# Two transformer blocks on one core: block 2's modulation product moved from the recurrence of block 1 to the spreading of the PEER gates

## The chip, the cores and the metric

The program runs on one core of a Trainium2 chip. The core has TensorE (PE in the profile, with PEld for its weight loads), VectorE (DVE), ScalarE (ACT), GpSimd (POOL) and SyncE (SP). SP issues most of the transfers between HBM and the on-chip memory; ACT and POOL issue some of their own. Each engine carries out its instructions in the order in which they stand in its stream. The metric is device time in microseconds (us), and lower is better.

## What is computed

512 tokens of 1024 features pass through two blocks. What matters here of the reference, cut:

```python
# block 1
mod = (silu(c) @ ada_w + ada_b)
shift1, scale1, gate1, shift2, scale2, gate2 = split(mod, 6)
h = rms_norm(x, norm1_g) * (1 + scale1) + shift1
...                       # attention (8 heads) and RWKV-7 delta rule (8 heads, both directions)
x = x + gate1 * mixed
h2 = rms_norm(x, norm2_g) * (1 + scale2) + shift2
x = x + gate2 * peer_ffn(h2)      # product keys, 16384 single-neuron experts
# block 2
mod = silu(c_2) @ w_ada + b_ada   # [1, 6144], needs c_2 alone
h = rmsnorm(x, norm_mix) * (1 + scale_m) + shift_m
...                       # retention, HGRN, GLA, output projection, experts
```

The modulation product of a block is a row of 1024 numbers times a matrix of 1024 x 6144 in float32 (24 MB). Block 2's needs nothing of block 1, and its result is first read when block 2 begins.

## The kernel before

**Order of the instructions.** The program is written as a sequence of tiles and operations. A scheduler that keeps a timeline of its own then fixes each engine's order; operations under `high_priority` go ahead of the others. [...] A tile pool with `bufs=n` has n buffers for a name or tag: a load into a buffer waits until the last reader of its earlier contents is done.

**Stages.** Times are of the profiled execution, from the span's start: projections of block 1 until 216 us; the recurrence (with the attention and the modulation as fillings) to 705; queries and top 16 of the PEER layer to 870; the spreading of the gates to 1147; the expert products to 2140; block 2.

**Modulation (`ada_parts`, lines 203 to 225).** A generator: each `next()` does one of 12 blocks of 512 columns. A block is 8 products (one for each row tile k of 128), each 32x512 in float32 on 128 rows. Row tile k goes to output partitions 32*(k % 4) on, so four neighbours use four column groups of the array. The weights (`adaw`, line 212) come in loads of two row tiles, 512 KB, with two buffers in the pools `wada2` and `wada3`. Line 214 is the product, `adaps` its PSUM tile. After the last block ACT copies the sum (`adarow`, line 219), PE transposes it (line 222), DVE adds the bias (line 224).

**Recurrence (`rwkv`).** For each of 4 pairs of heads: forward products within chunks of 64 steps (`pa`, `pvy`, `pq`), inverses on the lanes, `solve` (tiles `p`, `pm`, `pr`) for each direction, then `chain` (`pS`, lines 872 and 875), which walks over the 8 chunks, and `finish` (`mps`, `vps`). Pair j's forward stands beside pair j-1's backward work. `fill(j, k)` puts fillings between: `ADA[j][k]` blocks of modulation (8 of block 1, then 12 of block 2), attention steps (`sps`, `ptps`, `po`) and, for j = 4, tiles of the output projection (`zps`).

**Spreading (`spread(tt)`, three times 128 tokens).** A group is four tokens: DVE, POOL and ACT make one-hot tiles `oha` (with the gate) and `ohb`, PE multiplies them (`wps`, line 1169, four products), ACT copies the result into `wst` (line 1175), and every fourth group SP stores 1 MB (`wd`, or `wdr` for the last four). 32 groups make a `spread`. Each of `oha` and `ohb` has four buffers. `select(tt)` makes the indices; its transposes are `selps`. Beside it PE runs the first product (`ups`, 24 matmuls a tile) of 28 expert tiles, from loads `uraw`; POOL makes their low parts `ulo`.

**Expert products.** `vacc` from loads `vraw` (256 KB, four buffers), split by ACT into `vhi`, the rest into `vlo`. Their pools take the space of those of the spreading.

Of the kernel before, what the change touches and what calls it, by code (L numbers as in the profile page):

```python
# [40 lines left out]
def shape_consts():  # L41
    """Constants that depend on shapes alone."""
# [6 lines left out]
    # attention: distance and log of the number of patterns holding the offset  # L49
# [5 lines left out]
    # delta rule masks: two chunks of 64 on the partitions  # L55
# [31 lines left out]
def layout(I):  # L87
    """Data layout only: transposes, reshapes, concatenation."""
# [49 lines left out]
class K:  # L138
    def __init__(s, ctx, tc, nc, A):
# [10 lines left out]
        nc.vector.memset(s.onesD, 1.0 / D)  # L150
        s.mod = [cp.tile([128, 48], F32, name=f"mod{i}") for i in range(2)]
# [21 lines left out]
    def tables(s, after, name="natural_log_exp_and_others"):  # L173
        """one set of tables for what follows an activation, here both of log and exp"""
        with s.tc.issue_after(after.ins):
            s.nc.scalar.preload_act_table_set(name)

    def rsqrt(s, out, x, eps):
        """out = (x + eps) ** -0.5"""
        s.nc.scalar.activation(out, x, AF.Ln, bias=eps)  # L180
        s.nc.scalar.activation(out, out, AF.Exp, scale=-0.5)

    def rsqrt6(s, out, x, tmp, eps=1e-6, bias=None):
        """out = (x + eps) ** -0.5, with a step of Newton's method"""
# [6 lines left out]
    # ---------------------------------------------------------------- modulation  # L191
    def ada_begin(s, which, cname, pool):
        nc = s.nc
        sc = pool.tile([128, 8], F32, name=f"silu{which}")
        s.silu = nc.scalar.activation(sc, s.v(cname, 0, 8), AF.Silu)
        rep = pool.tile([128, 8, 43], F32, name=f"crep{which}")
        nc.gpsimd.memset(rep, 0.0)
        nc.vector.tensor_copy(rep[:, :, 11], sc)
        return rep

    def ada_parts(s, which, wname, bname, rep, lo, n, sel, wp, pp, tags=("mm", "tr"), spaces=None):
        """mod columns of the n column blocks (512 wide) from lo on, a block to each next(), two row tiles to a load.
        Block q goes to row q of each quarter, a quarter for every fourth row tile; its other rows get zeros."""
        nc = s.nc
        kn = 2
# [12 lines left out]
        row = wp().tile([128, 512], F32, name="adarow", bufs=1)  # L218
# [8 lines left out]
    # ------------------------------------------------- normalised, modulated input  # L227
    def rms(s, xT, wp, pp, tag="mm", ps=None):
        """rsqrt(mean(x*x) + eps)"""
# [12 lines left out]
    def modnorm(s, xT, r, gname, which, part, hhi, hlo, wp, keep=None):  # L242
        """h = x * r * (g * (1 + scale)) + shift, split in two parts."""
# [13 lines left out]
    def proj_tile(s, wsrc, hhi, hlo, wp, pp, eng=None, n=KT, tag="mm"):  # L257
        """One 128-column tile of the first n row tiles of h @ w, columns on partitions; returns the PSUM tile."""
# [11 lines left out]
    def out_proj(s, wname, mhi, mlo, xT, gatecol, wp, pp, ms=None, ahead=None, begun=0):  # L270
        """x += gate * (mix @ w) from tile begun on; the mean of its squares into ms; loads that run ahead of what follows"""
# [20 lines left out]
class Banks:  # L292
    """PSUM banks by tag"""
# [7 lines left out]
def block1(s, alloc, after):  # L301
    nc, tc, A = s.nc, s.tc, s.A
    mm = nc.tensor.matmul
    with ExitStack() as c1:
# [9 lines left out]
        sel = s.const("sel4", keep)  # L314
        rep = [s.ada_begin(0, "c", keep), s.ada_begin(1, "c2", keep)]
        s.tables(s.silu)

        with ExitStack() as c2:
# [3 lines left out]
            rest = itertools.chain(s.ada_parts(0, "ada_w", "ada_b", rep[0], 4, 8, sel, wada, P, ("ad", "ad")),  # L322
                                   s.ada_parts(1, "ada_w2", "ada_b2", rep[1], 0, 12, sel, wada, P, ("ad", "ad")))

            def room():
                """pools of what runs beside the recurrence"""
# [16 lines left out]
            def tail(forward):  # L343
                """the output projection of all but the last pair beside the last of the recurrence"""
# [8 lines left out]
                todo["late"] = ca = ExitStack()  # L353
                todo["wa"] = ca.enter_context(tc.tile_pool(name="wada3", bufs=2, side="right"))
# [14 lines left out]
            with ExitStack() as c3:  # L369
# [7 lines left out]
                for _ in s.ada_parts(0, "ada_w", "ada_b", rep[0], 0, 4, sel, lambda: wa, P, spaces=spaces):  # L377
# [5 lines left out]
                # token shift coefficient of the token itself  # L383
# [3 lines left out]
                for ct in [24, 25, 16, 12, 17, 18, 19, 13, 14, 15, 20, 21, 22, 23]:  # L387
# [9 lines left out]
                    if 4 <= j < 8:  # L397
                        # kk: normalised by head
# [45 lines left out]
            # the last pair  # L444
            x, wp, (mhi, mlo) = todo["x"], todo["w"], todo["mix"]
            todo["late"].close()
# [21 lines left out]
ATT = 4, 3, 3, 3     # steps of the attention to each filling  # L468
ADA = ((2, 0, 1, 1), (1, 1, 1, 1), (1, 1, 1, 0), (2, 1, 0, 0), (1, 2, 2, 2))    # parts of the modulation to each filling
OUT = 1, 2, 2, 3, 0  # tiles of the output projection to each filling  # L470


def attention(s, P, ap, qkd, vd, mixd):
    """softmax over the three patterns at once, two heads and 128 queries at a time; a step to each next()"""
# [45 lines left out]
def rwkv(s, c, P, zrd, mixd, kkd, sad, gd, room, fill, tail):  # L520
    """Both directions of the delta rule in chunks of 64 steps; the second runs on reversed time.
    Goes on with every next(): constants, gates, the first pair's decays, and the rest, which yields the last
    pair's part of the mix.

    Partitions hold two heads' features (e, f) or two chunks' steps (c, t).  A product that keeps
    the two apart contracts over all 128 partitions, one operand being zero outside its own half.
    """
# [8 lines left out]
    class Room:  # L536
        """a tile in the pool of its tag"""
# [1633 lines left out]
```

## Time and profile before

| what | value |
|---|---|
| median of 3 runs | 2857.38 us (2854.79 to 2861.47) |
| span of the profiled execution, first to last instruction | 2856.4 us |
| PE busy | 2586.5 us, 91% |
| DVE busy | 1999.3 us, 70% |
| mean granted clock of PE | 0.96 of full speed |

The profile gives no time of the profiled execution beside its span; the span lies between the lowest and the highest run, so what lies around it is small against the spread of the runs. Busy shares are means over stages with different limits, so they are read by stage. In a row of busy times, x is the number of instructions; a float32 matmul is two instructions. The number in brackets behind a row of the timeline is the engine's idle time just before it and what ended it.

### The profile page before, as it was taken

How to read it: one execution, taken by the hardware profiler on the slowest of the kernel's cores; microseconds unless marked ns; L12 is line 12 of the kernel's file. 1: busy time of each engine (PE TensorE's matmuls, PEld its weight loads, DVE VectorE, ACT ScalarE, POOL GpSimd, SP SyncE). 2: the span in 40 equal slices, each digit the busy share in tenths (PEclk: the TensorE clock that was granted, in tenths of full speed). 3: DMA queues.
4: the chain of work that ended last, by engine and by line, in shares of the span. 5: the costliest groups of instructions: out<-in, count | busy, mean ns of one | idle time of the engine just before them, and what ended most of it. 6: DMA issues, size and time to landing. Idle time of an engine off the chain costs nothing. (4 is left out here: it accounts for less than half of the span.)

```text
span 2856.4 us, 44680 instructions
## 1 busy us (share of the span) xinstructions
PE 2586.5 (91%) x16918; PEld 2042.6 (72%) x16918; DVE 1999.3 (70%) x3833; ACT 1059.1 (37%) x1946; POOL 1159.9 (41%) x860
## 2 busy tenths in 40 slices
PE   7999888987996786899999999999998999989995
PEld 4764456645886775889999999999986665654442
DVE  3666567544899999788888887878865467563323
ACT  3344434422434465333333333333333353231121
POOL 0012212121534666887776776776542223200002
PEclk9999999998998899999999999999999999889998
DMA  6528763451312465788888888887672222069984
GB/s 243 176 80 273 214 195 87 146 166 58 106 60 76 124 178 166 275 313 312 304 285 282 290 295 286 299 294 270 208 239 96 80 64 79 4 261 413 414 350 170
DMA packets 257160, 587.84 MB, mean 206 GB/s; under 512 B 48024, under 2 KB 120240, under 8 KB 246448
## 3 DMA queue, kind: packets, MB, share of 16 engines
q1 hardware_dynamic: 201856, 393.71, 40.2%
q0 software_dynamic: 38016, 138.43, 14.2%
q10 hardware_dynamic: 17072, 52.83, 5.0%
q8 instruction: 134, 2.20, 0.3%
q14 instruction: 82, 0.67, 0.1%
HBM read 529.05 MB, written 55.84 MB: 205 GB/s over the span
## 5 line engine op out<-in xcount | busy, mean ns | idle before, releaser
L165 PE MATMUL vacc<-gh,vhi 128*128 128x384 f32 x1024 | 346.6, 339 | 19.3 <-DVE xres L1343 13.9
L165 PE MATMUL ups<-phhi,uhi 128*128 128x384 f32 x1024 | 348.8, 341 | 10.4 <-ACT ge L1007 10.4
L167 PE MATMUL ups<-phhi,ulo 128*128 128x384 f32 x1024 | 348.3, 340 | 5.9 <-POOL ulo L171 4.3
L166 PE MATMUL ups<-phlo,uhi 128*128 128x384 f32 x1024 | 348.2, 340 | 1.0 <-DVE phlo L253 1.0
L166 PE MATMUL vacc<-gl,vhi 128*128 128x384 f32 x1024 | 344.8, 337 | 0.7 <-DVE gl L171 0.7
L167 PE MATMUL vacc<-gh,vlo 128*128 128x384 f32 x1024 | 325.6, 339 | 11.2 <-POOL vlo L171 10.2
L170 ACT ACTIVATE vhi<-vraw 128x512 fp32r<-128x512 f32 x256 | 160.2, 631 | 325.1 <-PE vacc L166 130.7
L170 ACT ACTIVATE uhi<-uraw 128x1024 fp32r<-128x1024 f32 x128 | 135.7, 1060 | 302.1 <-PE ups L166 258.7
L1227 DVE CUSTOM_DVE_ANT_0 row<-row,phtok 128x1024 f32<-128x1024 f32 x128 | 203.7, 1594 | 34.2 <-DMA row<-u_rows,peid 28.0
L171 POOL TENSOR_TENSOR vlo<-vraw,vhi 128x512 fp32r<-128x512 f32 x128 | 193.5, 1512 | 78.3 <-ACT vhi L170 71.4
L165 PEld LDWEIGHTS vacc<-gh,vhi 128*128 128x128 f32 x1024 | 194.1, 190 | 25.1 <-DVE xres L1343 18.0
L1232 DVE SCALAR_TENSOR_TENSOR acc<-row,dot,acc 128x1024 f32<-128x1024 f32 x127 | 192.4, 1515 | 19.5 <-DMA row<-peer_v,peid 19.4
L1218 POOL DMA_INDIRECT row<-peer_v,peid x128 | 170.5, 1332 | 86.0 <-DVE acc L1232 36.6
L165 PEld LDWEIGHTS ups<-phhi,uhi 128*128 128x128 f32 x1024 | 196.2, 192 | 10.9 <-ACT ge L1007 10.7
L167 PEld LDWEIGHTS vacc<-gh,vlo 128*128 128x128 f32 x1024 | 191.6, 190 | 15.8 <-POOL vlo L171 12.8
L167 PEld LDWEIGHTS ups<-phhi,ulo 128*128 128x128 f32 x1024 | 195.9, 191 | 7.7 <-POOL ulo L171 5.5
L166 PEld LDWEIGHTS ups<-phlo,uhi 128*128 128x128 f32 x1024 | 196.1, 192 | 1.5 <-DVE phlo L253 1.3
L166 PEld LDWEIGHTS vacc<-gl,vhi 128*128 128x128 f32 x1024 | 194.2, 190 | 1.4 <-DVE gl L171 1.2
L1275 POOL TENSOR_TENSOR ge<-ge,wg 128x384 f32<-128x384 f32 x124 | 162.5, 1319 | 75.2 <-DMA wg<-wdr 60.0
L1218 POOL DMA_INDIRECT row<-u_rows,peid x128 | 171.4, 1339 | 52.5 <-DVE dot L1227 20.5
L171 DVE TENSOR_TENSOR ulo<-uraw,uhi 128x1024 fp32r<-128x1024 f32 x100 | 141.8, 1418 | 45.6 <-ACT uhi L170 45.0
L171 DVE TENSOR_TENSOR vlo<-vraw,vhi 128x512 fp32r<-128x512 f32 x128 | 129.4, 1011 | 52.5 <-ACT vhi L170 50.3
(658 smaller groups left out, 5840.4 us busy)
## 6 DMA issues: line engine op xcount, KB each, us to landing
uraw<-peer_u SPq DMA_DIRECT2D x128, 512.0 KB
vraw<-peer_v SPq DMA_DIRECT2D x256, 256.0 KB
wgu<-w_gu SPq DMA_DIRECT2D x32, 2048.0 KB
adaw<-ada_w SPq DMA_DIRECT2D x96, 512.0 KB
wdn<-w_dn SPq DMA_DIRECT2D x32, 1024.0 KB
wd<-wst SPq DMA_DIRECT2D x20, 1024.0 KB
wg<-wd ACTq DMA_DIRECT2D x16, 1280.0 KB
wraw<-w_in SPq DMA_DIRECT2D x22, 512.0 KB
```

What stands on the lines that cost most here:

```text
L165: mm(ps, lhsT=L[0], rhs=R[0], start=first, stop=False)
L166: mm(ps, lhsT=L[0], rhs=R[1], start=False, stop=False)
L167: mm(ps, lhsT=L[1], rhs=R[0], start=False, stop=last)
L170: s.nc.scalar.activation(hi, x, AF.Copy)
L171: return (eng or s.nc.vector).tensor_tensor(lo, x, hi.bitcast(F32), OP.subtract)
L1218: nc.gpsimd.indirect_dma_start(out=r, out_offset=None, in_=(urows, vrows)[which], in_offset=bass.IndirectOffsetOnAxis(ap=eid[:, p:p + 1], ...
L1227: nc.vector.tensor_tensor_reduce(out=r, in0=r, in1=htok, scale=1.0, scalar=0.0, op0=OP.mult, op1=OP.add, accum_out=dot[:, p:p + 1])
L1232: nc.vector.scalar_tensor_tensor(acc, r, dot[:, p:p + 1], acc, OP.mult, OP.add)
L1275: i = (nc.vector if grp == 0 and e % 2 == 0 else nc.gpsimd).tensor_tensor(g3, g3, W[0][:, :, e, :], OP.mult)
```

## The change

Block 2's 12 blocks of modulation are no longer part of the recurrence's fillings. `ADA` now hands out the 8 blocks of block 1 alone, in its first three pairs. A second generator, `later`, is advanced in `spread`, at groups 4, 12, 20 and 28 of each of the three calls. Its loads hold one row tile (`kn=1`: 256 KB), from a pool `pada` of two buffers on the SP queue. For the space, `oha` and `ohb` have three buffers in place of four, and the PSUM banks of the stage are three for `mm`, two for `tr` and one for the modulation, where `mm` and `tr` had three each. The silu of both conditions is made at the start as before. Comments are gone from the file, which shifts the line numbers by up to six. The core of the diff:

```diff
-    def ada_parts(s, which, wname, bname, rep, lo, n, sel, wp, pp, tags=("mm", "tr"), spaces=None):
-        nc = s.nc
-        kn = 2
+    def ada_parts(s, which, wname, bname, rep, lo, n, wp, pp, tags=("mm", "tr"), spaces=None, kn=2, rows=None):
+        nc, (rep, sel) = s.nc, rep
...
-        row = wp().tile([128, 512], F32, name="adarow", bufs=1)
+        row = rows() if rows else wp().tile([128, 512], F32, name="adarow", bufs=1)
...
-            rest = itertools.chain(s.ada_parts(0, "ada_w", "ada_b", rep[0], 4, 8, sel, wada, P, ("ad", "ad")),
-                                   s.ada_parts(1, "ada_w2", "ada_b2", rep[1], 0, 12, sel, wada, P, ("ad", "ad")))
+            rest = s.ada_parts(0, "ada_w", "ada_b", rep, 4, 8, wada, P, ("ad", "ad"))
...
-ADA = ((2, 0, 1, 1), (1, 1, 1, 1), (1, 1, 1, 0), (2, 1, 0, 0), (1, 2, 2, 2))    # parts of the modulation to each filling
+ADA = ((1, 0, 1, 0), (1, 0, 1, 1), (1, 0, 1, 1), (0, 0, 0, 0), (0, 0, 0, 0))
...
-            pp1 = c1.enter_context(tc.tile_pool(name="pq", bufs=3, space=PSUM))
...
+            P = Banks(c1, tc, "pq", mm=3, tr=2, ad=1)
...
+            wa = c1.enter_context(tc.tile_pool(name="pada", bufs=2))
+            later = s.ada_parts(1, "ada_w2", "ada_b2", s.ada_begin(1, kp), 0, 12, lambda: wa, P, ("ad", "ad"), kn=1,
+                                rows=lambda: wp.tile([128, 512], F32, name="adarow", tag="oh", bufs=1))
...
-                    a = wp.tile([128, 4, 128], F32, name="oha", bufs=4)
-                    b = wp.tile([128, 4, 128], F32, name="ohb", bufs=4)
+                    a = wp.tile([128, 4, 128], F32, name="oha", bufs=3)
+                    b = wp.tile([128, 4, 128], F32, name="ohb", bufs=3)
...
                 for g in range(32 + 2):
+                    if g % 8 == 4 and g < 32:
+                        next(later)
```

How the instructions stand now is shown at three places. The first is PE in the recurrence, in the chain over the chunks of the third pair. Before:

```order
L872 MATMUL pS<-Sb_415,PB 64x64 x4
L875 MATMUL pS<-RP,Sb_415 64x64 x4
L214 MATMUL adaps<-adaw,crep_91 32x512 x2
L872 MATMUL pS<-Sb_416,PB 64x64 x4
L875 MATMUL pS<-RP,Sb_416 64x64 x4
L214 MATMUL adaps<-adaw,crep_91 32x512 x2
L875 MATMUL pS<-RP,Sb_415 64x64 x4
L744 MATMUL p_5890<-X,E 32x16 x32
L214 MATMUL adaps<-adaw,crep_91 32x512 x2
L889 MATMUL mps<-yacc,k_blk_62 128x512
```

The same place in the changed kernel, on the same engine:

```order
L868 MATMUL pS<-Sb_411,PB 64x64 x4
L871 MATMUL pS<-RP,Sb_411 64x64 x4
L868 MATMUL pS<-Sb_412,PB 64x64 x4
L871 MATMUL pS<-RP,Sb_412 64x64 x4
L871 MATMUL pS<-RP,Sb_411 64x64 x4
L740 MATMUL p_5770<-X,E 32x16 x32
L885 MATMUL mps<-yacc,k_blk_62 128x512
```

The pairs of modulation products between the steps of the chain are gone; all 48 pairs of block 2 leave the recurrence in this way.

The second place is the end of the spreading on PE. Before, the last groups follow each other and the expert products `vacc` come next:

```order
L165 MATMUL ups<-phhi,uhi 128x384
L166 MATMUL ups<-phlo,uhi 128x384
L167 MATMUL ups<-phhi,ulo 128x384
L1169 MATMUL wps<-oha,ohb 128x128 x156
L165 MATMUL vacc_10631<-gh,vhi 128x384
```

In the changed kernel (`crep_8030` is block 2's condition, `k_sel_8033` the selector of the transposes):

```order
L1163 MATMUL wps<-oha,ohb 128x128 x24
L213 MATMUL adaps<-adaw,crep_8030 32x512
L1163 MATMUL wps<-oha,ohb 128x128 x4
L213 MATMUL adaps<-adaw,crep_8030 32x512
L1163 MATMUL wps<-oha,ohb 128x128 x12
L213 MATMUL adaps<-adaw,crep_8030 32x512 x28
L221 MATMUL adaps_9679<-k_sel_8033,adarow 128x12 x4
L166 MATMUL ups<-phhi,uhi 128x384
```

Of the 96 products of block 2, 11 stand ahead of the first `wps`, 57 single or in twos among the 384 `wps` products (41 of them among the first 240), and 28 behind the last. Behind those stand the four transposes, 21 matmuls of the last `ups` tile, and then `vacc`.

The third place is the SP queue at the same point. Before:

```order
L1181 DMA wd<-wst 128x16x128 x6
L1184 DMA wdr<-wst 128x15x128 x3
L1322 DMA vraw<-peer_v 128x512 x2
L1184 DMA wdr<-wst 128x15x128
L1322 DMA vraw<-peer_v 128x512 x6
```

In the changed kernel:

```order
L1175 DMA wd<-wst 128x16x128
L211 DMA adaw<-ada_w 128x512 x2
L1178 DMA wdr<-wst 128x15x128
L211 DMA adaw<-ada_w 128x512 x2
L1178 DMA wdr<-wst 128x15x128
L211 DMA adaw<-ada_w 128x512
L1178 DMA wdr<-wst 128x15x128
L211 DMA adaw<-ada_w 128x512
L1178 DMA wdr<-wst 128x15x128
L211 DMA adaw<-ada_w 128x512 x26
L1318 DMA vraw<-peer_v 128x512 x14
```

One or two loads of the modulation stand behind each store of the spreading, 26 behind the last, and the loads `vraw` of the expert products behind those.

## Rows read from the trace of the kernel before

**Rows 1.** The page's first line.

```profile
span 2856.4 us, 44680 instructions
```

**Rows 2.** Busy time by stretch, columns PE, PEld, DVE, ACT, POOL, PEclk, DMA share, GB/s.

```profile
363.00:455.00 92.00, 81.76 (x1132) 47.46 (x1122) 60.13 (x183) 35.55 (x85) 18.95 (x16) 0.96 0.61 178
455.00:545.00 90.00, 81.44 (x1477) 61.57 (x1477) 72.30 (x230) 44.47 (x105) 16.06 (x14) 0.96 0.27 78
545.00:632.00 87.00, 69.77 (x891) 37.99 (x890) 36.09 (x108) 22.84 (x50) 15.41 (x12) 0.96 0.63 193
1147.00:2140.00 993.00, 964.08 (x5462) 951.41 (x5463) 821.10 (x896) 361.58 (x613) 693.33 (x507) 0.99 0.82 283
```

**Rows 3.** The same of the modulation's products alone (PE, PEld).

```profile
363.00:455.00 92.00, 23.30 (x96) 3.25 (x96) 0.96 0.61 178
545.00:632.00 87.00, 26.76 (x96) 3.55 (x96) 0.96 0.63 193
```

**Rows 4.** PE's waits in 363 to 455, then in 545 to 632: total us, times, longest.

```profile
PE adaps L214 <- DMA adaw<-ada_w: 7.4, 7, 2.5
...
PE adaps L214 <- DMA adaw<-ada_w: 13.4, 11, 2.1
```

**Rows 5.** Timeline of PE: first step of the chain for the first three pairs.

```profile
397.50 0.46 PE L872 MATMUL pS<-Sb,PB 128*64 128x64 f32 x8
...
491.20 0.46 PE L872 MATMUL pS<-Sb,PB 128*64 128x64 f32 x8
...
578.62 0.43 PE L872 MATMUL pS<-Sb,PB 128*64 128x64 f32 x5 [1.34 <-DVE Sb L866]
```

**Rows 6.** The modulation's products between those, by stretch (PE, PEld).

```profile
397.50:491.20 93.70, 15.52 (x56) 2.07 (x56) 0.96 0.42 124
491.20:578.60 87.40, 9.89 (x32) 1.21 (x32) 0.92 0.47 147
```

**Rows 7.** PE's waits in the same two stretches.

```profile
PE adaps L214 <- DMA adaw<-ada_w: 6.2, 5, 2.5
...
PE adaps L214 <- DMA adaw<-ada_w: 3.7, 2, 2.1
```

**Rows 8.** Timeline of PE: four products side by side, then two side by side.

```profile
330.99 1.06 PE L214 MATMUL adaps<-adaw,crep 128*32 128x512 f32 x8
331.99 0.44 PE L694 MATMUL pa<-ar,bd 128*64 128x128 f32 x4
...
597.84 1.05 PE L214 MATMUL adaps<-adaw,crep 128*32 128x512 f32 x4 [1.91 <-DMA adaw<-ada_w]
598.82 0.46 PE L875 MATMUL pS<-RP,Sb 128*64 128x64 f32 x8
```

**Rows 9.** Busy time in the spreading, up to its 240th product and after; columns as Rows 2.

```profile
899.40:1075.80 176.40, 141.17 (x895) 134.01 (x893) 176.26 (x199) 101.21 (x216) 114.81 (x79) 0.94 0.48 142
1075.80:1143.20 67.40, 42.88 (x288) 36.24 (x288) 65.23 (x71) 34.95 (x75) 45.57 (x35) 0.97 0.58 165
```

**Rows 10.** PE's longest wait in 899.4 to 1075.8.

```profile
PE selps L1134 <- DVE selp L1123: 13.6, 3, 6.4
```

**Rows 11.** Timeline of SP: loads of 512 KB through two buffers.

```profile
595.30 22.23 SPq L212 DMA_DIRECT2D adaw<-ada_w  x8
```

**Rows 12.** Timeline at the end of the spreading: PE, then SP, then ACT.

```profile
1141.98 1.16 PE L1169 MATMUL wps<-oha,ohb 128*128 128x128 f32 x8 [0.89 <-POOL oha L1154]
1147.47 1.65 PE L165 MATMUL vacc<-gh,vhi 128*128 128x384 f32 x4 [4.33 <-ACT vhi L170]
...
1143.21 0.82 SPq L1322 DMA_DIRECT2D vraw<-peer_v  x2
1144.13 0.38 SPq L1184 DMA_DIRECT2D wdr<-wst  x1
...
1146.79 0.63 ACT L170 ACTIVATE vhi<-vraw 128x512 fp32r<-128x512 f32 x1 [1.47 <-DMA vraw<-peer_v]
```

More of the change, by code (lines that the diff above doesn't have):

```diff
@@ L150, in __init__ @@
         nc.vector.memset(s.onesD, 1.0 / D)
+        s.csilu = cp.tile([128, 2, 8], F32, name="csilu")
         s.mod = [cp.tile([128, 48], F32, name=f"mod{i}") for i in range(2)]
@@ L189, in rsqrt6, with ada_begin @@
         stt(out, tmp, 1.5, out, OP.add, OP.mult)
-    def ada_begin(s, which, cname, pool):
+    def ada_begin(s, which, pool):
         nc = s.nc
-        sc = pool.tile([128, 8], F32, name=f"silu{which}")
-        s.silu = nc.scalar.activation(sc, s.v(cname, 0, 8), AF.Silu)
         rep = pool.tile([128, 8, 43], F32, name=f"crep{which}")
         nc.gpsimd.memset(rep, 0.0)
-        nc.vector.tensor_copy(rep[:, :, 11], sc)
-        return rep
-    def ada_parts(s, which, wname, bname, rep, lo, n, sel, wp, pp, tags=("mm", "tr"), spaces=None):
-        nc = s.nc
-        kn = 2
+        nc.vector.tensor_copy(rep[:, :, 11], s.csilu[:, which])
+        return rep, s.const("sel4", pool)
+    def ada_parts(s, which, wname, bname, rep, lo, n, wp, pp, tags=("mm", "tr"), spaces=None, kn=2, rows=None):
+        nc, (rep, sel) = s.nc, rep
         ps = pp.tile([128, 512], F32, name="adaps", tag=tags[0])
@@ L313, in block1 @@
         vd = dp.tile([4, 128, 4, 128], F32, name="vd")
-        sel = s.const("sel4", keep)
-        rep = [s.ada_begin(0, "c", keep), s.ada_begin(1, "c2", keep)]
-        s.tables(s.silu)
+        for i, n in enumerate(("c", "c2")):
+            silu = nc.scalar.activation(s.csilu[:, i], s.v(n, 0, 8), AF.Silu)
+        rep = s.ada_begin(0, keep)
+        s.tables(silu)
         with ExitStack() as c2:
@@ L352, in tail @@
                 todo["w"] = wp
-                todo["late"] = ca = ExitStack()
-                todo["wa"] = ca.enter_context(tc.tile_pool(name="wada3", bufs=2, side="right"))
                 def out():
@@ L376, in block1 @@
                 spaces = itertools.cycle([(wa, "adaw"), (wp, "wraw"), (wa, "adaw"), (wp, "whi"), (wa, "adaw"), (wp, "wlo")])
-                for _ in s.ada_parts(0, "ada_w", "ada_b", rep[0], 0, 4, sel, lambda: wa, P, spaces=spaces):
+                for _ in s.ada_parts(0, "ada_w", "ada_b", rep, 0, 4, lambda: wa, P, spaces=spaces):
                     pass
@@ L445, in block1 @@
             x, wp, (mhi, mlo) = todo["x"], todo["w"], todo["mix"]
-            todo["late"].close()
             rp = after.enter_context(tc.tile_pool(name="b1r", bufs=1, side="right"))
@@ L804, in rwkv @@
         class Pair:
+            pass
         def begin(j):
@@ L1012, in peer @@
         with ExitStack() as c1:
-            pp1 = c1.enter_context(tc.tile_pool(name="pq", bufs=3, space=PSUM))
-            class PP:
-                def tile(self, shape, dt, name, tag):
-                    return pp1.tile(shape, dt, name=name, tag=tag)
-            P = PP()
+            P = Banks(c1, tc, "pq", mm=3, tr=2, ad=1)
             kp = c1.enter_context(tc.tile_pool(name="pk", bufs=1))
@@ L1559, in block2_mix @@
                 class Feat:
+                    pass
                 def prepare(j):
@@ L1670, in block2_mix @@
             class Pair:
+                pass
             def scores(f, pr):
```

## The prediction

> **What bounds the kernel now.** The span is 2856.4 us [rows 1]. I first split it into stages by the table of busy time by stretch, because the mean shares hide that the limit changes. In the two stretches of the recurrence where block 2's modulation runs, PE is busy 81.8 of 92 us and 69.8 of 87 us, DVE 60.1 and 36.1 [rows 2]: PE is the fullest engine, but not full. In the spreading it is the other way round: up to the 240th `wps` product DVE is busy 176.26 of 176.40 us and PE 141.2 [rows 9]. In the expert products PE is busy 964 of 993 us [rows 2], so whatever delays their start delays the end by the same amount.
>
> Then I looked at what the moved work occupies. Block 2's 96 products are 192 instructions; they sit in 363 to 455 and 545 to 632 and nowhere else (96 instructions in each), with 23.3 and 26.8 us of PE [rows 3]. The list of waits adds that PE stands still in front of them, waiting for their loads, for 7.4 and 13.4 us [rows 4].
>
> **The change, part by part.**
>
> *Taken out of the recurrence.* The products hold PE for 23.3 + 26.8 + 7.4 + 13.4 = 70.9 us. That is the upper bound of the return, reached if PE alone paced the stage. How much comes back can be read from two neighbouring intervals, from one pair's chain to the next: 397.5 to 491.2 lasts 93.7 us, 491.2 to 578.6 lasts 87.4 [rows 5]. The first holds 15.5 + 6.2 = 21.7 us of products and waits, the second 9.9 + 3.7 = 13.6 [rows 6, 7]. 8.1 us less of it made the interval 6.3 us shorter, a rate of 0.78. Two intervals are a thin basis, and their other work is not the same. In the last part, from 595 on, there is no forward work left: there the chain's own steps through DVE and ACT would show between PE's instructions once the fillers are gone. In 545 to 632 PE without the products has 43 us of work for 87, so the rate must be lower. I take 0.65: a return of 46 us, with 35 (a half) and 70.9 as bounds. Block 1's eight blocks stay, and their DVE, ACT and POOL work is unchanged.
>
> *Put into the spreading, on PE.* In the recurrence the products went out in twos and fours. Two side by side hold PE from 597.84 to 598.82, 0.98 us, and four from 330.99 to 331.99, 1.00 us [rows 8]. The time does not depend on how many go together, since each uses its own column group. The new loads hold one row tile, and the order sets most products singly. No row shows one alone; it lies between half of a pair, 0.49, and a pair, 0.98, and since four cost as much as two I take 0.98. Up to the 240th `wps` 41 products are added: 40 us. PE's 141.2 us become 181, in a stretch of 176.4. Some waits can't be filled: the 13.6 us in which the transposes `selps` wait for DVE's reduction [rows 10] stay, as everything behind them on PE waits too. That gives 195, or 18 us more than now. DVE can't work ahead meanwhile, since `oha` and `ohb` have three buffers, so its 100% no longer hides PE. Below: products that meet in twos and filled waits leave 4 us. Above: all of the present 35 us of idle PE time stays, 141.2 + 40 + 35 = 216, 40 us more. I take 18. After the 240th product PE has 42.9 us of work in 67.4 [rows 9]; 16 more products make 59, so there is no cost there, as DVE covers it; without that cover it would be 16 us. The 11 products ahead of the first `wps` lie beside DVE's top 16 and are taken as nothing too.
>
> *Put behind the spreading.* 26 loads stand on SP behind the last store, with 28 products behind the last `wps` on PE, and the expert products' loads and matmuls behind those. With two buffers a load can't be issued before the product two places earlier is done, so the pace is half of (load to use, plus product). For 512 KB loads, eight issues lie in 22.23 us [rows 11], 3.13 us apart, so load to use is 2 x 3.13 - 0.98 = 5.3 us. The nearest row for 256 KB is the first `vraw`: issued at 1143.21, used at 1146.79, 3.6 us, with a store in flight, as it will be here [rows 12]. This gives (3.6 + 0.98) / 2 = 2.3 us a load, 59 us for 26. If all of a load's time went with its size it would be 2.65 us, a pace of 1.8 and 47 us; if none did, 3.1 and 81. I take 59, as the row has the size and the company. Nothing hides it: from the last `wps` to the first `vacc` PE now waits 4.33 us [rows 12], and the expert products are PE's. ACT's copy, the four transposes and 21 late `ups` matmuls run while the first `vraw` comes in, which takes those 4 us as before; I add 2 us for what doesn't overlap. Together 61 us.
>
> The Trainium skill (DMA: Bandwidth & Descriptors, on the two cost components) gives a transfer a fixed part of about 2.0 us and the rest by its size, 436 GB/s. By it 256 KB would take 2.6 us and 512 KB 3.2; halving a load saves little, which speaks against loads half as large. The 5.3 us of the trace for 512 KB, two in flight, is far above its 3.2. With 2.6 us the 26 loads would cost 47 us, and the sum below would come to 2877.
>
> *The rest.* The POOL fill and the DVE copy of the condition move by one instruction each; two PSUM banks in place of three for the transposes: each is emptied by one ACT copy, and DVE, not PE, sets the pace there. Nothing for these. A head start of DVE and POOL in the tail is worth nothing either, as PE is busy 97% of the expert stage.
>
> Sum: 2856.4 - 46 + 18 + 61 = 2889 us. The span lies 1 us below the median of the runs, 2857.38, so the same figure stands for the median.
>
> **The rivals.** About 0.2%, 6 us, is what a measurement of this kernel can tell from no change.
>
> *Faster: PE's time comes back whole and is covered whole.* PE alone paces the recurrence (return 70.9) and DVE stays the only limit of the spreading (cost 0), leaving the tail: 2856.4 - 70.9 + 61 = 2847. For it: PE is the fullest engine of the recurrence, and the rate 0.78 is not far from 1. Against it: 43 us of PE work left in 87, and PE's 181 us in a stretch of 176.4. It decides once return less stretch exceeds 67. Chance 0.10.
>
> *No change.* Return at 0.78 (55 us) and a tail at 47 + 2 with a stretch of 4 to 10: 2855 to 2860. Chance 0.08.
>
> *Dearer: PE becomes the limit of the spreading.* With in-order waits for loads that stand on SP behind a store, all idle time of PE stays: 40 in place of 18, 2911, and up to 2933 if the tail runs at 3.1 us a load. For it: 181 us of work in 176.4, and a third buffer less. Against it: the loads are issued some groups ahead of their use. Chance 0.20.
>
> *The forecast,* 2863 to 2905: chance 0.62.
>
> **How the numbers follow.** The likeliest gives 2889. The dearer case reaches to 2930; the 0.10 of the faster case stays mostly below 2850, and what lies above 2930 is about as likely. So the range is 2850 to 2930. Faster by over 0.2% is the first rival, 0.10; within it the second, 0.08; slower is the rest, 0.82.
>
> **What would show it.** Right: the chain of the third pair (`pS`) starts some 25 us earlier than 578.6, and the last `lops` some 46 earlier; behind the last `wps` some 25 products each with a wait for `adaw`, 2.3 us apart, and `vacc` 60 us or more after the last `wps`; in the spreading DVE no longer at 100% but waiting for PE, and single products 0.98 us apart from the next instruction. Wrong: a tail below 40 us (loads faster than any row here), a recurrence that is shorter by 65 or more, or DVE still at 100% through the spreading.

## The result, and the profile after

The changed kernel takes 2944.64 us (median of 4 runs, 2936.54 to 2947.29), the kernel before 2857.99 beside it: a ratio of 1.0301 with an interval of 1.0282 to 1.0319. It is slower, as forecast, but by 87 us in place of 31, and outside the range. Executions of one program differ by about 1% (twelve of the version at the end of experiment 6 took 2841 to 2877 us, the longer ones at a lower mean granted clock), and so do the stages in two profiles.

The page's first line of the profiled execution, against [rows 1]:

```profile
span 2944.8 us, 44750 instructions
```

So 88.4 us of span have to be found. I follow them in the order of the program, by the marks that the prediction used.

**Recurrence.** Timeline of PE, the first chain steps of the four pairs (answering [rows 5]; the fourth started at 671.4 before):

```profile
405.10 0.73 PE L868 MATMUL pS<-Sb,PB 128*64 128x64 f32 x6 [4.23 <-DVE Sb L862]
...
483.58 0.70 PE L868 MATMUL pS<-Sb,PB 128*64 128x64 f32 x8
...
573.76 0.74 PE L868 MATMUL pS<-Sb,PB 128*64 128x64 f32 x7 [5.14 <-DVE Sb L862]
...
661.97 0.43 PE L868 MATMUL pS<-Sb,PB 128*64 128x64 f32 x5 [2.01 <-DVE Sb L862]
```

The first chain starts 7.6 us later than before, the second 7.6 earlier, the third 4.8, the fourth 9.4. The output products behind the recurrence (`lops`), before and after, in the list by tile (smallest, median and largest duration in ns, then the first and the last start):

```profile
L165 PE MATMUL lops<-mhi,whi x8: 397/710/796, 694.3 to 703.8; 128*128 128x512 f32 x8
```

```profile
L166 PE MATMUL lops<-mhi,whi x8: 397/710/796, 686.7 to 696.1; 128*128 128x512 f32 x8
```

The first starts at 686.7 in place of 694.3: in this profile 7.6 us came back, not 46. Six of the versions in the experiments have the same recurrence as the changed kernel, and there it ends at 674.3 to 682.9. So this profile is the longest of seven, and the return is better given as 8 to 20 us.

What took the rest is seen in the busy time by stretch, first of the changed kernel (columns as [rows 2]), then the last stretch of the kernel before, which the front does not show:

```profile
363.00:455.00 92.00, 76.31 (x1258) 55.83 (x1259) 71.31 (x207) 41.22 (x96) 23.66 (x20) 0.94 0.24 62
455.00:545.00 90.00, 81.48 (x1267) 59.48 (x1271) 67.69 (x212) 40.91 (x97) 13.49 (x12) 0.89 0.24 69
545.00:632.00 87.00, 68.50 (x1034) 51.97 (x1033) 43.93 (x119) 26.65 (x57) 21.64 (x15) 0.82 0.25 74
632.00:705.00 73.00, 56.24 (x407) 40.02 (x406) 29.87 (x74) 18.08 (x28) 11.09 (x5) 0.81 0.15 50
```

```profile
632.00:705.00 73.00, 62.32 (x547) 46.57 (x546) 30.61 (x76) 19.55 (x32) 17.36 (x8) 0.88 0.18 62
```

In 545 to 632, where 26.8 us of products went out [rows 3], PE is busy 68.5 us against 69.8 [rows 2], and the sixth number, the granted clock, is 0.82 against 0.96. A mean of 0.82 means that part of the stretch ran at the lower of PE's two levels, 1.2 GHz. Some earlier work has moved into the stretch, so the whole stage is the fair measure. Busy time from 216 us to the first `lops`, all instructions and then the modulation's alone, before and after:

```profile
216.00:694.30 478.30, 417.81 (x5275) 253.80 (x5273) 283.80 (x819) 181.80 (x404) 100.33 (x79) 0.95 0.53 164
216.00:694.30 478.30, 87.97 (x336) 13.51 (x336) 0.45 (x2) 1.21 (x2) 0.95 0.53 164
```

```profile
216.00:686.70 470.70, 399.52 (x5074) 264.97 (x5073) 291.93 (x818) 182.24 (x403) 101.94 (x79) 0.90 0.37 114
216.00:686.70 470.70, 36.76 (x136) 5.68 (x136) 0.21 (x1) 0.62 (x1) 0.90 0.37 114
```

The modulation's PE time fell by 88.0 - 36.8 = 51.2 us, as it should. But the rest of PE's work, the first row less the second, grew from 329.8 to 362.8 us, 33.0 more for the same instructions, and PE's idle time from 60.5 to 71.2, 10.7 more. 51.2 - 33.0 - 10.7 is 7.5, the 7.6 that came back. Of the 33.0, 6.6 are time in which a product and another instruction ran at once (11.0 us before, 4.4 after, by the times of the single instructions), so the other instructions alone hold PE for 26.4 us more. The chain's own products go with the lower clock: the median `pS<-Sb,PB` took 222 ns before and 270 after. The same two rows of own_row, the first experiment, whose recurrence is the same:

```profile
216.00:678.70 462.70, 389.91 (x5082) 261.30 (x5080) 293.74 (x819) 182.17 (x403) 103.64 (x79) 0.92 0.38 116
216.00:678.70 462.70, 34.61 (x136) 5.59 (x136) 0.20 (x1) 0.60 (x1) 0.92 0.38 116
```

Here the rest takes 25.5 us more than before and idle time 12.3. Over the seven profiles the rest takes 22 to 33 us more, PE is idle for 8 to 12 us more, and the granted clock of the stage is 0.90 to 0.93 against 0.95.

**Selection and spreading.** From the `lops` to the first `wps` the kernel takes 210.1 us against 205.1, from the first to the last `wps` 250.2 against 243.7. Busy time up to the 240th product and after it, answering [rows 9]:

```profile
896.80:1080.90 184.10, 174.49 (x989) 135.53 (x988) 148.87 (x189) 99.83 (x214) 101.77 (x75) 0.97 0.65 196
1080.90:1147.00 66.10, 55.87 (x321) 36.97 (x321) 63.94 (x70) 35.20 (x77) 45.66 (x35) 1.00 0.78 229
```

PE is now full (174.5 of 184.1) and DVE no longer (148.9): the limit has changed engines, as forecast, for 8 us in this part.

**Behind the spreading.** In the kernel before the first expert product followed the last `wps` by 4.3 us [rows 12]; now by 101.6. PE's timeline there:

```profile
1145.80 1.16 PE L1163 MATMUL wps<-oha,ohb 128*128 128x128 f32 x8 [0.89 <-POOL oha L1148]
1146.88 1.20 PE L213 MATMUL adaps<-adaw,crep 128*32 128x512 f32 x4
1153.81 2.51 PE L213 MATMUL adaps<-adaw,crep 128*32 128x512 f32 x4 [5.72 <-DMA adaw<-ada_w]
...
1212.20 1.05 PE L213 MATMUL adaps<-adaw,crep 128*32 128x512 f32 x2 [0.57 <-DMA adaw<-ada_w]
1214.27 1.04 PE L213 MATMUL adaps<-adaw,crep 128*32 128x512 f32 x2 [1.03 <-DMA adaw<-ada_w]
...
1217.63 1.06 PE L221 MATMUL adaps<-k_sel,adarow 128*128 128x12 f32 x8 [0.69 <-ACT adarow L218]
1242.22 0.69 PE L166 MATMUL ups<-phhi,uhi 128*128 128x384 f32 x1 [23.53 <-ACT ge L1003]
...
1248.61 0.34 PE L166 MATMUL vacc<-gh,vhi 128*128 128x384 f32 x1
```

Up to 1217 it is the picture of the forecast: products behind their loads, 70 us for 26 loads, 2.7 us each. Then comes a hole of 23.5 us that the forecast does not have. The other engines in that time (DVE, POOL, SP, ACT by their names in the rows):

```profile
1216.98 0.60 ACT L218 ACTIVATE adarow<-adaps 128x512 f32<-128x512 f32 x1 [69.05 <-PE adaps L213]
...
1218.88 2.29 DVE L1113 TENSOR_TENSOR oh<-ab,k_iota 128x2048 f32<-128x2048 f32 x1
1221.31 4.49 POOL L1116 TENSOR_TENSOR oh<-oh,xf 128x2048 f32<-128x2048 f32 x1 [38.57 <-DVE oh L1113]
...
1237.44 0.29 DVE L1124 SCALAR_TENSOR_TENSOR peid<-selp 128x128 int32<-128x128 f32 x1
1237.83 11.57 SPq L1318 DMA_DIRECT2D vraw<-peer_v  x6
1237.97 3.83 ACT L171 ACTIVATE gh<-ge 128x384 fp32r<-128x384 f32 x9 [20.39 <-DVE peid L1124]
```

`adarow`, the row that closes the modulation, is allocated under the tag `oh` with one buffer. That is the buffer in which `select` makes its comparison. `spread(2)`, which now ends with `adarow`, stands ahead of `select(3)`, so the selection of the last token tile, which ended at about 1020 us before, waits for the last product: `oh` twice, POOL's 4.49 us twice, `peid`, and only then the space of the stage is free for the value rows on SP.

**Expert stage.** Its busy time, against the last of [rows 2]:

```profile
1248.60:2219.60 971.00, 952.51 (x5437) 942.64 (x5437) 788.42 (x880) 354.91 (x598) 659.77 (x482) 1.00 0.82 281
```

It takes 971.0 us in place of 991.1, PE 952.5 busy: DVE and POOL had gated several groups in the tail, and 21 `ups` matmuls stand ahead of its start. 20 us come back here. From there to block 2's first gate-and-up product (`gups`) it takes 424.9 us against 417.5; the profiles of the twelve kernels below lie between 413.7 and 427.4, and no part of the change is there, so I count those 7 us as the spread between executions.

The account: -7.6 (recurrence), +5.0 (up to the first `wps`), +6.5 (spreading), +97.3 (tail), -20.1 (expert stage), +7.4 (behind it) is 88.4, up to rounding.

### The profile page after: what moved, and what is told of

Read it like the earlier page. It is cut to its first block, busy times and chain, and to the rows that moved or that the text cites. A ratio compares the mean times of both kernels' runs of the same rounds, so it can differ in the third digit from the quotient of the medians.

```text
span 2944.8 us, 44750 instructions
## 1 busy us (share of the span) xinstructions
PE 2664.1 (90%) x16918; PEld 2061.5 (70%) x16918; DVE 1971.3 (67%) x3833; ACT 1058.4 (36%) x1946; POOL 1153.0 (39%) x860
## 5 line engine op out<-in xcount | busy, mean ns | idle before, releaser
L166 PE MATMUL ups<-phhi,uhi 128*128 128x384 f32 x1024 | 347.8, 340 | 23.5 <-ACT ge L1003 23.5
L172 POOL TENSOR_TENSOR vlo<-vraw,vhi 128x512 fp32r<-128x512 f32 x128 | 200.4, 1566 | 91.0 <-ACT vhi L171 76.8
L213 PE MATMUL adaps<-adaw,crep 128*32 128x512 f32 x384 | 150.8, 675 | 64.3 <-DMA adaw<-ada_w 64.2
L1271 POOL TENSOR_TENSOR ge<-ge,wg 128x384 f32<-128x384 f32 x124 | 149.3, 1211 | 94.2 <-DMA wg<-wdr 67.9
```

What stands on the lines that cost most here:

```text
L166: mm(ps, lhsT=L[0], rhs=R[0], start=first, stop=False)
L172: return (eng or s.nc.vector).tensor_tensor(lo, x, hi.bitcast(F32), OP.subtract)
L213: nc.tensor.matmul(ps[32 * j:32 * j + 32, :], lhsT=rep[:, k, 11 - q:43 - q], rhs=w[:, k % kn, :], start=q == 0 and k < 4, stop=q == n - 1 ...
L1271: i = (nc.vector if grp == 0 and e % 2 == 0 else nc.gpsimd).tensor_tensor(g3, g3, W[0][:, :, e, :], OP.mult)
```

## The experiments

Ratios are to the kernel before in the same series, with their interval. Two versions of different series are compared by their medians, and by their ratios where the two disagree; "tail" is the time from the last `wps` to the first `vacc`.

**1. own_row.** The closing row gets a buffer of the loads' pool.

```diff
-                                rows=lambda: wp.tile([128, 512], F32, name="adarow", tag="oh", bufs=1))
+                                rows=lambda: wa.tile([128, 512], F32, name="adarow", tag="adaw"))
```

> The changed kernel, with the row that ends block 2's modulation in a buffer of the loads' own pool and no longer in the one that the last token tile's selection uses. Theory (the selection of tile 3 waits in line for that row, and it alone puts 31 us behind the last product, 1217 to 1248.6 us): tile 3's expert numbers are made before 1025 us again, the first expert product starts 23 to 31 us sooner (1218 to 1226), and the time is 2913 to 2922 us. Rival (the 31 us are the transfers of the value rows, which start only when the spreading's space is free, so that another row buffer changes nothing): first expert product within 5 us of 1248, time 2940 to 2947.

2919.74 us, ratio 1.0258 (1.0232 to 1.0285). DVE's timeline has the expert numbers back beside the spreading, and ACT's tail goes straight from the row to the gates (`gh`):

```profile
984.86 2.47 DVE L1124 SCALAR_TENSOR_TENSOR peid<-selp 128x128 int32<-128x128 f32 x1
```

```profile
1211.09 0.60 ACT L218 ACTIVATE adarow<-adaps 128x512 f32<-128x512 f32 x1 [65.53 <-PE adaps L213]
1213.70 3.83 ACT L171 ACTIVATE gh<-ge 128x384 fp32r<-128x384 f32 x9 [2.02 <-PE adaps L221]
```

The tail is 79.6 us in place of 101.6. The median time is 25 us less, but the two were measured in different series, and by their ratios the difference is 12 us (1.0301 less 1.0258). That the shared buffer makes the hole is shown, and the rival is out; its price lies between 12 and 25 us.

**2. after_no_mod2 and before_no_mod2.** Block 2's modulation is left out in either kernel, which keeps its own places for block 1.

```diff
-            later = s.ada_parts(1, "ada_w2", "ada_b2", s.ada_begin(1, kp), 0, 12, lambda: wa, P, ("ad", "ad"), kn=1,
-                                rows=lambda: wp.tile([128, 512], F32, name="adarow", tag="oh", bufs=1))
+            nc.vector.tensor_copy(s.mod[1], s.v("ada_b2", 0, 48))
...
-                    if g % 8 == 4 and g < 32:
-                        next(later)
```

> The changed kernel without block 2's modulation product at all: its 48 columns are the bias alone (left out: 96 loads of 256 KB and the products on them). Theory (the recurrence gives back some 8 us only, since TensorE's granted clock falls to 0.82 once the products are gone, and everything else that the change costs lies behind the gates' spreading): end of the recurrence as in the changed kernel (687 us), last gate product at about 1132, first expert product 5 us behind it, and 2845 to 2852 us, 6 to 12 below the kernel before. Rival of the forecast (the recurrence returns 35 to 70 us when nothing else is in its way): 2785 to 2820.

> The kernel before, block 2's modulation product left out (its 48 columns are the bias alone), and the eight remaining blocks of block 1 at their old places, as the old table gives them out. Theory (the new table's places for block 1, not the lost fillers, put the first chain 7.6 us later): the first chain starts at or before 397 us, the second and the later ones earlier by the whole of what products and waits took there, so the recurrence ends at 660 to 675 and the time is 2825 to 2845. Rival (it is the clock: without fillers TensorE is granted 0.82 and the recurrence pays the products' time back): recurrence ends at 682 to 690 and 2842 to 2852 us.

after_no_mod2: 2848.54 us, ratio 0.9990 (0.9975 to 1.0006), in the range of its theory. In its profile (2832.5 us; the other twelve executions took 2844.8 to 2855.4) the recurrence ends at 674.3, where I expected 687. before_no_mod2: 2839.68 us, ratio 0.9957 (0.9943 to 0.9972), first chain at 390.4, end at 668.4. So the whole of block 2's products, and all that they wait for, are worth 12 to 15 us to the kernel before, and 3 to 7 with the new table: the forecast's 46 is refuted even with nothing put anywhere else. Both theories for before_no_mod2 hold in part. Its rows from 216 us to the first `lops`:

```profile
216.00:668.40 452.40, 383.99 (x5077) 256.26 (x5075) 288.90 (x818) 181.20 (x403) 101.58 (x79) 0.91 0.39 118
216.00:668.40 452.40, 37.74 (x136) 5.75 (x136) 0.21 (x1) 0.61 (x1) 0.91 0.39 118
```

Of 50.2 us of modulation that are gone, PE's other work takes 16.4 more and its idle time 7.9 more; 25.9 come back in this execution. The chain intervals are 80.5, 85.7 and 86.4 us against 93.7, 87.4 and 92.8: the first gives 13, the second hardly anything, the third 6.

**3. before_mod2_resident and before_mod2_twice.** The products stay in the recurrence but read a resident tile; in the second each is issued twice.

```diff
-                if k % kn == 0:
+                if which:
+                    w = s.ident[:, None, None, :].to_broadcast([128, kn, 4, 128])
+                elif k % kn == 0:
...
+                for r in range(1 + which):
```

> The kernel before with block 2's 96 products at their old places, but on a resident tile, so that their 48 loads of 512 KB and the waits for them are gone and TensorE's work stays (its modulation's values are thereby not the reference's). Theory (the products of the second half of the recurrence cost their waits of 3.7 to 13.4 us a stretch and hold the clock up besides): granted clock 0.95 or more from 455 to 705 us, recurrence ends 12 to 30 us sooner than the 694.3 of the kernel before, time 2827 to 2846. Rival (waits are slack that the chain would spend anyway): within 5 us of 2858.

> before_mod2_resident with each of block 2's products issued twice (192 in place of 96, on a resident tile; the values are not the reference's). Theory (TensorE's queue is short of a us in the recurrence only in part: taking the 96 out gave 12 to 26 us for some 45 us of TensorE's time, because idle time and a lower granted clock took the rest): adding 96 lengthens the recurrence by 12 to 26 us, time 2870 to 2884. Rival (one for one, TensorE bounds every stretch and its clock has no more to give): 40 to 50 us longer, 2897 to 2908. Other rival (all slack): within 5 us of 2858.

Resident: 2857.87 us, ratio 1.0016 (0.9990 to 1.0042). Taking out the loads and their waits gave nothing back; my theory there was wrong, and the 20.8 us of waits [rows 4] that stood in the upper bound of 70.9 were no part of the return. Twice: 2879.09 us, ratio 1.0104 (1.0075 to 1.0134), in the range of the theory of a part price. From 216 us to the first `lops`, resident and then twice, all work and then the modulation's:

```profile
216.00:694.70 478.70, 416.12 (x5280) 269.25 (x5279) 287.30 (x819) 181.98 (x404) 100.17 (x79) 0.91 0.37 112
216.00:694.70 478.70, 61.95 (x336) 12.60 (x336) 0.44 (x2) 1.23 (x2) 0.91 0.37 112
```

```profile
216.00:714.60 498.60, 439.23 (x5467) 271.68 (x5465) 288.06 (x819) 181.99 (x404) 101.89 (x79) 0.93 0.36 107
216.00:714.60 498.60, 97.55 (x528) 21.60 (x528) 0.45 (x2) 1.23 (x2) 0.93 0.36 107
```

In resident all products stay, yet their PE time is 62.0 us in place of 88.0, the rest of PE's work takes 24.4 us more at a granted clock of 0.91 in place of 0.95, and the stage is as long as before. Over whole executions the mean clock is 0.945 to 0.954 in resident and 0.953 to 0.964 in the kernel before beside it. So a lower clock does not need the products to be gone, and the waits are not tested alone here. Twice, set against resident, is the mirror image of taking out: 35.6 us of products more, 12.5 us less for the other work at a higher granted clock (0.93), 3.2 us less idle, 19.9 us longer.

**4. early_parts, three_loads, three_loads_shared_row.** Is the tail a matter of where parts are given out, or of the room for loads? First own_row with all parts in the first two tiles:

```diff
-                    if g % 8 == 4 and g < 32:
+                    if tt < 2 and g % 5 == 2 and g < 32:
```

then own_row, and the changed kernel itself, with a third buffer:

```diff
-            wa = c1.enter_context(tc.tile_pool(name="pada", bufs=2))
+            wa = c1.enter_context(tc.tile_pool(name="pada", bufs=3))
```

> own_row with the twelve parts given out in the first two tiles' spreading, six each, and two loads in flight as before. Theory (the ring of two loads sets the pace, not the place where a part is given out): products still stand behind the last gate product (22 by the order of the program), the tail is 55 to 70 us and the time 2905 to 2922. Rival (the parts are given out too late): tail gone, 2860 to 2880.

> own_row with room for three 256 KB loads of block 2's modulation weights in place of two. Theory (what leaves 25 to 28 products behind the spreading is the ring of two small loads, each of which is asked for only when the product two before it is through; with a third all 96 products find a place before the last gate product): last gate product to first expert product 4 to 12 us, the expert stage back to about 990 us since nothing is done ahead in a tail, the spreading 5 us longer than in own_row for the products that move into it; together 2860 to 2875 us. Rival (in the spreading the loads are held by the gate stores and the gathers on the same engines, so that more loads in flight only wait longer): products and gate products wait, the spreading takes 40 to 60 us more, 2895 to 2920.

> The changed kernel with three loads in flight and nothing else, so the closing row still lies in the buffer that the selection of tile 3 uses. Theory (two causes in line, the ring of loads and the shared buffer): one product is left behind the spreading, and the selection of tile 3 still stands behind the closing row, so that the last gate product to the first expert product takes 25 to 35 us and the time is 2880 to 2895. Rival (the shared buffer costs only when the products are late): 4 to 12 us, as three_loads.

early_parts: 2919.71 us in one run, the same time as own_row, with 22 products behind the last `wps` and a tail of 71.7 us, somewhat over the 55 to 70 expected. three_loads: 2872.26 us, ratio 1.0061 (1.0040 to 1.0083), with the end of the spreading as in [rows 12]:

```profile
1159.22 1.16 PE L1163 MATMUL wps<-oha,ohb 128*128 128x128 f32 x8 [0.89 <-POOL oha L1148]
1164.80 1.65 PE L166 MATMUL vacc<-gh,vhi 128*128 128x384 f32 x4 [4.42 <-ACT vhi L171]
```

One buffer of 256 KB removes the tail. It is not the transfers that were too slow for the spreading: the order of PE and SP is fixed when the program is built, and with two buffers of 256 KB it sets 22 to 28 products behind the last `wps`, wherever the parts are given out, with three one at most. The spreading is 265.4 us, 10 longer than own_row's where I expected 5, and the expert stage is back at 990.2. three_loads_shared_row: 2895.86 us in one run. One product is left behind the last `wps`, and the selection still stands in line behind the row:

```profile
1153.66 0.60 ACT L218 ACTIVATE adarow<-adaps 128x512 f32<-128x512 f32 x1 [0.38 <-PE adaps L213]
...
1158.91 2.93 DVE L1113 TENSOR_TENSOR oh<-ab,k_iota 128x2048 f32<-128x2048 f32 x1
...
1182.94 0.61 DVE L1124 SCALAR_TENSOR_TENSOR peid<-selp 128x128 int32<-128x128 f32 x1
```

A tail of 41.2 us, somewhat over the 25 to 35 expected, and a time just over the range. So the shared buffer costs something with the late products and without them: 22 us of tail and 12 to 25 of time with them, 37 us of tail and 24 of time (one run) without, where the spreading is 9 and the expert stage 6 us shorter than in three_loads.

**5. two_large_loads.** Two loads of 512 KB in flight, own row buffer.

```diff
-            later = s.ada_parts(1, "ada_w2", "ada_b2", s.ada_begin(1, kp), 0, 12, lambda: wa, P, ("ad", "ad"), kn=1,
-                                rows=lambda: wa.tile([128, 512], F32, name="adarow", tag="adaw"))
+            later = s.ada_parts(1, "ada_w2", "ada_b2", s.ada_begin(1, kp), 0, 12, lambda: wa, P, ("ad", "ad"), kn=2,
+                                rows=lambda: wa.tile([128, 2, 512], F32, name="adarow", tag="adaw")[:, 0])
...
-                sel = wp.tile([128, 3, 128], F32, name="selp")
+                sel = wp.tile([128, 3, 128], F32, name="selp", bufs=1)
```

> own_row with block 2's weights in 48 loads of 512 KB, two in flight, in place of 96 of 256 KB (one selection buffer fewer makes the space). Theory (what leaves products behind the spreading is how much weight is in flight, not the number of buffers or of parts): no products behind the last gate product, 2862 to 2880, as three_loads. Rival (a large load holds up the gate stores and the other loads on its engines): spreading more than 20 us longer than own_row's, 2885 or more.

2857.67 us in one run, 4 us under the range of the theory; no tail (4.4 us), and a spreading of 253.3 us, 12 shorter than three_loads'. The products' own PE time up to the 240th `wps` tells why, first three_loads, then two_large_loads:

```profile
895.00:1092.50 197.50, 56.98 (x127) 7.48 (x126) 0.00 (x0) 0.00 (x0) 0.99 0.71 209
```

```profile
892.20:1080.20 188.00, 36.49 (x140) 4.87 (x140) 0.00 (x0) 0.00 (x0) 0.95 0.76 230
```

A load of two row tiles brings its two products side by side: 140 instructions hold PE for 36.5 us, 0.26 each; singly, 127 hold it for 57.0, 0.45 each. It is the pair of [rows 8] against the lone product that no row there showed.

**6. The table, and versions that might beat both.** three_loads_old_table and two_large_old_table take the old table for block 1's blocks, as the cut below shows; shared_out has a table of its own, leaves eight of block 2's blocks in the recurrence and puts four into the spreading.

```diff
-ADA = ((1, 0, 1, 0), (1, 0, 1, 1), (1, 0, 1, 1), (0, 0, 0, 0), (0, 0, 0, 0))
+ADA = ((2, 0, 1, 1), (1, 1, 1, 1), (1, 1, 1, 0), (2, 1, 0, 0), (1, 2, 2, 2))
```

> three_loads with block 1's eight blocks given out by the old table. Theory (the new table's places, not the lost fillers, put the first chain some 10 us later: 400 to 405 us in the three kernels with it against 390 in before_no_mod2): first chain at 388 to 393 us, end of the recurrence at 668 to 676, and 6 to 12 us below three_loads: 2850 to 2868, which is the kernel before within 0.4%. Rival (the first chain's start differs from execution to execution by as much): the same time as three_loads within 3 us.

> Block 2's modulation divided: none of it in the third row of the old table (the stretch before the first chain and its first interval, which took 93.7 us in the kernel before and 78 to 80 without products), eight of its blocks in the last two rows as in the kernel before, four in the spreading with two small loads in flight and an own row buffer, block 1's blocks by the old table. Theory (a product in the recurrence costs what it takes from a chain's interval: 14 us in the first and 7 us before it, 1 to 5 in the later ones, where it also keeps TensorE's clock; in the spreading 0.2 to 0.3 us each and no tail as long as the loads keep up): first chain at 388 to 393, end of the recurrence 665 to 682, spreading and selection 6 to 10 us longer than before, tail 4 us, time 2836 to 2852 against 2855. Rival (the recurrence spends the time anyway: granted clock and idle time take back what the first interval gives): end of the recurrence 686 or later, 2855 to 2870.

> two_large_loads with block 1's eight blocks given out by the old table: the version that the runs so far point to. Theory (the old table's places are worth some 10 us, as between three_loads and three_loads_old_table, and two large loads leave no tail and 250 to 256 us of spreading): first chain at 388 to 393 us, end of the recurrence 666 to 676, 2842 to 2854 us, which is 0 to 0.5% below the kernel before. Rival (the first chain's start is set by something else, as its 407 us in shared_out would have it, and the 10 us are not there again): 2855 to 2868.

three_loads_old_table: 2862.00 us, ratio 1.0025 (1.0003 to 1.0047), first chain at 390.5, end of the recurrence at 669.7. shared_out: 2858.33 us, ratio 1.0008 (0.9982 to 1.0033), and its theory failed at its first mark: the first chain starts at 406.8, for products of block 2 are set ahead of it although its third row of the table is empty (248 of the modulation's instructions before the first chain, as in the kernel before, against 208 in before_no_mod2). The recurrence ends at 692.9, as its rival has it. two_large_old_table: 2848.24 us, ratio 0.9986 (0.9957 to 1.0015), first chain at 393.1. Three pairs that have block 2's products out of the recurrence and differ in the table alone (without block 2's modulation, three loads, two large loads) stand 8.9, 10.3 and 9.4 us apart in their median times (two_large_loads with one run), and the first chain starts at 390.4 to 393.1 with the old table against 398.8 to 406.0 in the seven profiles with the new one: the new places of block 1's parts cost some 9 us. With block 2's products in the recurrence as well, the old table's first chain starts at 397.5 to 416.3, in before, shared_out, resident and twice, so the table alone does not set it. The best version found has a median below the kernel before, but an interval that holds 1.

## Why the prediction was wrong, step by step

- **"I take 0.65: a return of 46 us", bounds 35 and 70.9.** This step failed: 7.6 us in the changed kernel's profile, 8 to 20 over the seven with its recurrence, 3 to 7 in the time of after_no_mod2, below the lower bound. The products' PE time did go (51 us). What was not asked is what the engine does without them: its granted clock was lower, the same remaining work took 33 us more, and 11 us of idle time appeared. The rate read from two neighbouring intervals did not hold: without the products the second interval got only 1.7 us shorter in before_no_mod2. The waits for loads should not have counted as a return: taking the loads out changed the time by nothing that can be told (before_mod2_resident). And "block 1's eight blocks stay" was taken as free, while their new places cost 9 us.
- **"Put into the spreading, on PE", 18 us.** Right in mechanism and about in size: DVE's 100% fell to 81%, PE became the fuller engine, and selection and spreading together grew by 11.5 us. 5 of them lie ahead of the first `wps`, where the prediction put 11 products and took them as nothing: from the `lops` to the first `wps` it is 209 to 214 us in the nine profiles that have products there and 202 to 209 in the five that have none. The lone product at nearly the price of a pair is borne out by experiment 5.
- **"Nothing hides it ... Together 61 us".** Half right. The products' part was mis-sized a little: 2.7 us a load in place of 2.3, 70 us in place of 59, inside its bounds. What failed is "I add 2 us for what doesn't overlap": the hole is 23.5 us, and 22 us of tail and 12 to 25 of time go with the buffer in own_row, because the row shares a buffer with the selection behind it. The diff shows the tag; the argument followed PE and SP alone, and the selection that it delays is DVE's and POOL's.
- **"By it 256 KB would take 2.6 us".** This estimate was worked out from the Trainium skill (DMA: Bandwidth & Descriptors, "Anatomy of one DMA — SWDGE (gpsimd) path", the two cost components), a section on transfers that GpSimd issues, while SP issues these. From issue to landing, min, median and max, first 256 KB loads (own_row, from 880 us on), then 512 KB loads (two_large_loads):

```profile
DMA to landing us min/median/max: 2.5/3.2/8.0
```

```profile
DMA to landing us min/median/max: 3.8/5.1/8.6
```

  Its 2.6 and 3.2 us are nearly the minimum of the first and lie below that of the second; the medians beside other transfers are 3.2 and 5.1, and the measured times decide.
- **"A head start ... is worth nothing".** Failed by 20 us to the other side: 970 to 974 us for the expert stage in the changed kernel, own_row and early_parts, whose tails are 72 to 102 us, 982 to 993 in the others. Of the changed kernel's 20 us, 10 are idle time of PE (28.5 us before, 18.5 after) and 10 are PE's busy time, of which the 21 `ups` matmuls that ran ahead of the start are at most 6.4 (1242.2 to 1248.6).
- **"No change" and "faster" as rivals** fell with the return; "dearer" was right on the sign of the miss but for another reason than PE in the spreading.

What stays open: how much of the 33 us is the clock alone, and whether the missing products are what lowered it (no run here held the clock while taking the products out, and in before_mod2_resident it fell with the products in place); and why a table that gives block 1's parts out in other fillings starts the first chain 9 us later.

## What to carry to other kernels

Work that fills a stage's holes is not worth its own time when it leaves: here 50 us of PE time gave 12 to 26 back in the best case, and doubling the same work cost 20 to 25, so price a removal by what the rest will do at the clock and with the holes that remain. When a new tile takes an existing tag, list who uses that buffer next and where it stands in the program, on every engine. And a fixed order with a small ring of loads can put work behind a stage whatever place the code gives it: room for one more load was worth some 47 us here, a shift of the places none (one run).

## What the hardware showed beyond that

In the first 47 us of the tail, while TensorE did little but wait for loads, its granted clock was 0.60 (both levels mixed), and one product that ran by itself (at 1170.35) took 1.91 us; from 1194 on, at 0.93, ten of twelve took 1.04 or 1.05 us. That product, then windows of the changed kernel:

```profile
1170.35 1.91 PE L213 MATMUL adaps<-adaw,crep 128*32 128x512 f32 x2 [2.66 <-DMA adaw<-ada_w]
```

```profile
1147.00:1194.00 47.00, 20.91 (x32) 2.64 (x31) 4.36 (x4) 0.90 (x2) 20.45 (x20) 0.60 0.59 204
1194.00:1217.00 23.00, 13.96 (x24) 1.69 (x24) 0.00 (x0) 0.02 (x1) 0.00 (x0) 0.93 0.42 129
```
